# A decoder layer's feed forward: low parts of the right factors on GpSimd, output shares two units later, two last outputs from ScalarE's queue

## The chip, the core and the metric

One core of a Trainium2 chip runs the whole kernel in one launch. The metric is the device time of one execution in microseconds; the median of several runs counts. The engines are TensorE (PE; its weight loads are PEld), VectorE (DVE), ScalarE (ACT), GpSimd (POOL) and SyncE (SP), whose queue issues nearly all DMAs.

## The reference

One inference step of a decoder layer, for a prompt of 512 tokens and 8 sample tokens, with a width of 1024. All is float32.

```python
def run_trunk(x, pos, ...):
    mix, s_new, kvs = token_mixer(rmsnorm(h, ln1_g), pos, ...)
    h = h + mix
    h = h + swiglu(rmsnorm(h, ln2_g), w_ffn_in, w_ffn_out)
    y = rmsnorm(h, lnf_g)

def swiglu(xn, w_ffn_in, w_ffn_out):
    a, b = jnp.split(xn @ w_ffn_in, 2, axis=-1)
    return (jax.nn.silu(a) * b) @ w_ffn_out
```

The mixer (retention, dilated window attention, gates) fills the first 930 us of the kernel. The change lies in `swiglu`, whose hidden width is 2816 (22 blocks of 128), and in the final norm.

## The kernel before, in words

All activations stand transposed, channels on partitions, the 520 tokens as columns in two halves of 260. Every float32 product is made of three products of rounded parts: a value is split into a high part, rounded by ScalarE (`A.activation(..., AF.Copy)` into the type fp32r), and a low part, value minus high part, by VectorE; the three products are high by high, high by low and low by high. The weights come from `wall` in the order of use, 512 KB a DMA on SP's queue, are split the same way (`wh` by `block_hi` at L201, `wl` at L204) and run some five blocks ahead of TensorE (`advance`).

The feed forward goes by units, one for each of the 22 hidden blocks. A plain unit (`ffn_in`) makes the two products `a` and `b` one after the other, 96 matmuls of 128x260. The others, listed in `INQ`, are quads (`ffn_in_quad`): the two output blocks, the two token halves and pairs of weight blocks are taken as a 2x2 product made with seven block products in place of eight, 84 matmuls. Each quad needs three sums of weights from VectorE (`block_sum`, L185, L189 and L191), which are then split as well, and factors of the activations on the right. The seven blocks of a quad go to three PSUM banks: blocks 1, 3, 5, 7 to one, 2 and 6 to another, 4 to a third (`SEVEN`). After blocks 1, 2, 3 and 5 ScalarE copies the bank to SBUF (`s`, L313), since the next block of that bank adds to it; a block therefore waits for that copy. VectorE evacuates the rest: `fa` at L1368 after blocks 4 and 6, `uf` at L1376 after block 7.

The hidden activations `uf` of two neighbouring units are what the output products read. `right(b, k)` makes the right factors of a pair: four VectorE instructions make the sums `us`, and three pieces (`uf`, 780 columns; `us`, 520 columns, twice) are split, high parts `UH` by ScalarE at L1314, low parts `UL` by VectorE at L1318. It is a generator on the track `"S"`; each `pump` of the matmul loop lets it take one step, so its instructions are strewn over the unit after.

The hidden blocks stand in three chunks of 8, 8 and 6 (`CHUNKS`). When a chunk is done, its share of the output is made: four quads `ffn_out(0)`, `(2)`, `(4)`, `(6)`, each adding to two blocks of `hT`. `FFSEQ` gives the order. The shares of a chunk stand one unit behind its last unit, so that `right` has that unit to run in: units 0 to 8, four shares, units 9 to 16, four shares, units 17 to 21, then the last chunk's outputs in plain products (`LAST`), whose factors `whole` splits without sums. Units 7, 8, 9, 11, 12, 13, 15, 16, 17, 19, 20 and 21 are quads.

Right factors of a full pair are made behind the odd units 3, 5, 7, 9, 11, 13 and 15 and, for the first pair, behind unit 2. Units 3 to 6 run beside `gen_factors`, which makes the quads' factors of the normalised input (`XP`, `XT`) on VectorE and ScalarE.

At the end, `fin_out(f)` scales the rows of each token half and stores them: for each of two column halves, row block `j` even by VectorE, `j` odd by ScalarE, each followed by a DMA on SP's queue, then the small `y_s`.

Of the kernel before, what the change touches and what calls it, by code (L numbers as in the profile page):

```python
# [11 lines left out]
ALU = mybir.AluOpType  # L12
# [10 lines left out]
NFF = 22  # L23
# [4 lines left out]
INQ = (7, 8, 9, 11, 12, 13, 15, 16, 17, 19, 20, 21)  # L28
FFSEQ = []
for (a_, n_), ahead_ in zip(CHUNKS, (1, 1, 0)):  # L30
    FFSEQ += [("in", i_, i_ in INQ) for i_ in range(a_ and a_ + 1, a_ + n_ + ahead_)]
    FFSEQ += [("out", c_, True) for c_ in range(0, 8, 2) if ahead_]
QUADS = {128 + 2 * i_: 4 for i_, e_ in enumerate(FFSEQ) if e_[2]}
SCW = (8, 7, 7, 6)
# [4 lines left out]
def tile_hybrid_layer(  # L39
# [9 lines left out]
    V, A, G_, PE, SP = nc.vector, nc.scalar, nc.gpsimd, nc.tensor, nc.sync  # L49
# [13 lines left out]
    def halves(ap):  # L63
        return ap.rearrange("p (f c) -> p f c", f=2)
# [10 lines left out]
    def f32(ap):  # L75
        return ap.bitcast(F32)
# [28 lines left out]
    def later(n, fn):  # L105
        delayed.append([n, fn])
# [31 lines left out]
    def push(name, gen):  # L138
        tracks[name].append(gen)
        return gen  # L140

    def finish(name, gen):
        while gen in tracks[name]:
            run_delayed()
            step(name)
# [140 lines left out]
    def quad(factor, snap, evac):  # L286

        s = pos[0] // 8
        pos[0] += 16
        nkp = QUADS[s]  # L290

        turn["busy"] ^= 1
        pms = {}
        for _ in range(2):
            i = turn["next"]
            pms[i] = bank_pair(i)[:, 0, :HF]
        out = [pms[turn["busy"]], pms[1 - turn["busy"]], None]
        begun = set()
        for j, (bank, x) in enumerate(SEVEN):
            advance(bid[s, 0] + j)  # L300
            if bank == 2:
                out[2] = abank("pc")[:, :HF]
            h, l = split[bid[s, 0] + j]
            for k in range(nkp):
                ks = slice(k * 128, k * 128 + 128)
                for w, i in ((h, 0), (h, 1), (l, 0)):
                    PE.matmul(out[bank], w[:, ks], factor(i, k, x), start=bank not in begun, stop=k == nkp - 1 and w is l,  # L307
                              skip_group_check=True)
                    begun.add(bank)
                if k % 2:  # L310
                    pump()
            if j in (0, 1, 2, 4):
                A.activation(snap[(0, 3, 1, None, 2)[j]], out[bank], AF.Copy)  # L313
            evac(j, out[bank])
# [12 lines left out]
    def rstd_rows(pool, ssq, rows, ncol, n, tag):  # L327

        v = pool.tile([128, 8], F32, tag=tag + "v", bufs=2, name="v")
        V.tensor_scalar(v[:rows, :ncol], ssq, 1.0 / n, EPS, op0=ALU.mult, op1=ALU.add)  # L330
        r = pool.tile([128, 8], F32, tag=tag + "r", bufs=2, name="r")
        G_.tensor_tensor(r[:rows, :ncol], v[:rows, :ncol], mhalf[:rows].to_broadcast([rows, ncol]), op=ALU.pow)  # L332
        return r
# [831 lines left out]
    def ftmp(name):  # L1165
        return fp.tile([128, C], F32, tag="t", bufs=5, name=name)
# [101 lines left out]
    UF = {}  # L1268
    NP = CHUNKS[2][0]
    NX = 3  # L1270

    def snaps():
        return [fp.tile([128, 2, HF], F32, tag=t, bufs=b, name=t) for t, b in (("s12", 1), ("s35", 1))]

    def whole(i, t):
        hi, lo = (halves(u[:, i - NP, :]) for u in (UHp, ULp))
        A.activation(hi, t, AF.Copy)
        later(2, lambda: V.tensor_tensor(lo, t, f32(hi), op=ALU.subtract))

    def middle(i, mult):  # L1280

        if i > NP:
            t = halves(ftmp("fu"))
            mult(t)
            whole(i, t)
            return
        if i % 2 == 0:
            if len(rights) > 1:
                finish("S", rights[-2])
            UF[i // 2] = fp.tile([128, 4, HF], F32, tag="uf", bufs=2, name="uf")  # L1290
        t = UF[i // 2]
        mult(t[:, 1:3, :] if i % 2 else t[:, 0::3, :])
        if i == NX - 1:
            rights.append(push("S", right(UF[0], 0)))
        if i % 2 and i > NX - 1:
            rights.append(push("S", right(t, i % 8 // 2)))

    rights = []

    def right(b, k):  # L1300

        yield
        t = fp.tile([128, 4, HF], F32, tag="us", name="us")
        V.tensor_tensor(t[:, 0, :], b[:, 0, :], b[:, 3, :], op=ALU.subtract)
        yield
        V.scalar_tensor_tensor(t[:, 1, :], b[:, 2, :], -1.0, t[:, 0, :], op0=ALU.mult, op1=ALU.subtract)
        yield
        V.tensor_tensor(t[:, 2, :], b[:, 2, :], b[:, 3, :], op=ALU.subtract)
        yield
        V.scalar_tensor_tensor(t[:, 3, :], t[:, 1, :], -1.0, b[:, 1, :], op0=ALU.mult, op1=ALU.subtract)  # L1310
        yield
        for x, j, n in ((b[:, 0:3], 0, 3), (t[:, 0:2], 3, 2), (t[:, 2:4], 5, 2)):
            hi, lo = (u[:, k, j:j + n, :] for u in (UH4, UL4))
            A.activation(hi, x, AF.Copy)  # L1314
            yield
            if k < 3:
                yield
            V.tensor_tensor(lo, x, f32(hi), op=ALU.subtract)  # L1318
            if k < 3:
                yield  # L1320

# [60 lines left out]
    def ffn_out(c):  # L1382

        s12, s35 = snaps()
        h1, h2 = halves(hT[:, c, :]), halves(hT[:, c + 1, :])

        def evac(j, bank):
            if j == 3:
                V.tensor_tensor(h1[:, 0, :], bank, h1[:, 0, :], op=ALU.add)
                later(1, lambda: V.tensor_tensor(h1, h1, s12, op=ALU.add))  # L1390
            elif j == 4:
                later(1, lambda: V.tensor_tensor(s35[:, 0, :], s35[:, 0, :], s35[:, 1, :], op=ALU.add))
            elif j == 5:
                V.tensor_tensor(h1[:, 1, :], bank, h1[:, 1, :], op=ALU.add)
                V.tensor_tensor(h2[:, 1, :], h2[:, 1, :], s35[:, 0, :], op=ALU.subtract)
            elif j == 6:
                V.tensor_tensor(h2[:, 0, :], h2[:, 0, :], bank, op=ALU.subtract)

        quad(ufactor, [s12[:, 0, :], s12[:, 1, :], s35[:, 0, :], s35[:, 1, :]], evac)

    for kind, i, seven in FFSEQ:
        if kind == "out":
            if i == 0:
                finish("S", rights[-1])
            ffn_out(i)
            continue
        if i == NP + 1:
            whole(NP, UF[NP // 2][:, 0::3, :])
        (ffn_in_quad if seven else ffn_in)(i)

    last = bpool.tile([128, 7 * D], F32, tag="bg", name="last")
    yt = last[:, :4 * D].rearrange("p (j c) -> p j c", j=4)
# [4 lines left out]
    def fin_T(c, f):  # L1417
        h = hT[:, c, :]
        sp, sp2 = sbank(), sbank()
        for j in range(2):  # L1420
            o = f * HF + 128 * j
            pe_T(sp[:, j * 128:(j + 1) * 128], h[:, o:o + 128])
        pe_T(sp2[:4, :128], h[:, f * HF + HT:(f + 1) * HF])
        return sp, sp2

    def fin_ss(f, sq, first):
        for j in range(2):
            PE.matmul(ssb[:, 2 * f + j:2 * f + j + 1], sq[:, 128 * j:128 * j + 128], ones1, start=first and f + j == 0,
                      stop=not first, skip_group_check=True)
        PE.matmul(ssb[:4, 4 + f:5 + f], sq[:, HT:HF], ones1, start=False, stop=not first, skip_group_check=True)  # L1430
# [28 lines left out]
    def fin_out(f):  # L1459
        sq = ftmp("sqf")  # L1460
        A.activation(sq[:, :HF], hT[:, 7, f * HF:(f + 1) * HF], AF.Square)
        fin_ss(f, ssa[:, f * HF:(f + 1) * HF], True)
        a = fin_T(7, f)
        fin_ss(f, sq, False)
        r = rstd_rows(fp, ssb[:, 2 * f:2 * f + 2], 128, 2, D, "nf")
        r4 = rstd_rows(fp, ssb[:4, 4 + f:5 + f], 4, 1, D, "ng")
        fin_g(7, f, *a)
        for i in range(2):
            cs = slice(512 * i, 512 * i + 512)
            for j in (2 * f, 2 * f + 1):  # L1470
                if j % 2:
                    A.activation(yt[:, j, cs], yt[:, j, cs], AF.Copy, scale=r[:, 1:2])
                else:
                    V.tensor_scalar(yt[:, j, cs], yt[:, j, cs], r[:, 0:1], None, op0=ALU.mult)
                SP.dma_start(y_p[0, j * 128:(j + 1) * 128, cs], yt[:, j, cs])
        V.tensor_scalar(ys[:, f, :], ys[:, f, :], r4[:4, 0:1], None, op0=ALU.mult)
        SP.dma_start(y_s[4 * f:4 * f + 4].rearrange("r o d -> r (o d)"), ys[:, f, :])

# [26 lines left out]
    for f in range(2):  # L1505
        for c in range(4, 8):
            o = free_pair()[:, :1, :]
# [120 lines left out]
```

## Time and profile before

| | us |
|---|---|
| median of 3 runs (lowest to highest) | 1306.59 (1304.96 to 1307.02) |
| the profiled execution's own time | 1305.23 |
| its span, first to last instruction | 1303.4 |
| TensorE busy in the span | 1276.1 |
| VectorE busy | 821.0 |
| ScalarE busy | 573.5 |
| GpSimd busy | 83.6 |

The granted TensorE clock is 0.996 of full speed over the span. The profile is of one execution. The timeline lists instructions of one engine in order, with start and length in us and, in brackets, the idle time ahead and what ended it. Matmuls are pipelined: each is shown with some 0.28 us and the next starts 0.12 us later, so that an idle time shown ahead of a matmul is some 0.16 us less than the time that the stream lost. VectorE's instructions overlap a little at their ends; what one costs is the step from its start to the next one's.

### The profile page before, as it was taken

What the parts mean: (1) busy time and instruction counts of PE and PEld (TensorE: products, weight loads), DVE (VectorE), ACT (ScalarE), POOL (GpSimd) and SP (SyncE); (2) the same over time, 40 slices, a digit from 0 to 9 for tenths busy, and PEclk for the clock granted to TensorE, in tenths of its full rate; (3) what the DMA queues carried; (4) which work ended last, traced back from release to release, by engine and by line L of the source; (5) the groups of instructions that cost most, each with busy time, mean ns of one, the idle gap of its engine ahead of it and who ended that gap; (6) DMA issues with size and microseconds to landing.
All of it is one profiled execution on the core that took longest, in us unless ns stands there. A gap on an engine that the chain in (4) does not pass through costs nothing.

```text
span 1303.4 us, 25688 instructions
## 1 busy us (share of the span) xinstructions
PE 1276.1 (98%) x10465; PEld 1245.0 (96%) x10465; DVE 821.0 (63%) x1737; ACT 573.5 (44%) x1100; POOL 83.6 (6%) x69
## 2 busy tenths in 40 slices
PE   8999999999999999999999999999999999999997
PEld 7999999999898999999999999899999999999997
DVE  7866636847765532234545455476688988798765
ACT  4465334635563522244434343233354555555542
POOL 3601001001002000000000000040000000000000
PEclk8999999999999999999999999999999999999999
DMA  6266344746584332435555545624222333233321
GB/s 213 93 208 230 119 158 140 250 153 230 171 292 149 98 95 84 138 122 159 159 150 157 160 149 189 222 98 147 82 82 82 98 112 100 87 93 113 98 82 66
DMA packets 89782, 183.35 MB, mean 141 GB/s; under 512 B 12024, under 2 KB 33944, under 8 KB 89664
## 3 DMA queue, kind: packets, MB, share of 16 engines
q1 hardware_dynamic: 88944, 180.64, 43.0%
q8 instruction: 82, 1.34, 0.4%
q10 hardware_dynamic: 720, 1.07, 0.3%
q14 instruction: 36, 0.29, 0.1%
HBM read 155.70 MB, written 25.98 MB: 139 GB/s over the span
## 4 chain that ended last, share of the span: by engine, by line
PE 85%; DVE 6%; DMA 3%; issue 2%; ACT 2%; POOL 1%; SPq 1%; DVEq 0%; ACTq 0%
PE pm L251 61%; PE pm L307 10%; PE sp L323 3%; PE pc L307 2%; PE sp L553 2%; DVE wl L204 2%; PE sp L572 1%; DMA vb<-vd 1%; PE pm L1516 1%; PE sp L968 1%; ACT wh L201 1%; PE sp L505 1%; DMA out<-st 1%; PE sp L918 1%; PE sacc L1113 1%
## 5 line engine op out<-in xcount | busy, mean ns | idle before, releaser
L251 PE MATMUL pm<-X,wh 128*128 128x260 f32 x3392 | 560.9, 287 | 4.4 <-DVE X L355 3.6
L251 PEld LDWEIGHTS pm<-X,wh 128*128 128x128 f32 x3392 | 469.5, 189 | 18.9 <-issue 9.1
L204 DVE TENSOR_TENSOR wl<-raw,wh 128x512 fp32r<-128x512 f32 x384 | 274.4, 716 | 165.0 <-ACT wh L201 161.6
L251 PE MATMUL pm<-X,wl 128*128 128x260 f32 x1696 | 342.3, 283 | 0.0
L201 ACT ACTIVATE wh<-raw 128x512 fp32r<-128x512 f32 x384 | 238.7, 625 | 210.7 <-PE pm L251 163.5
L251 PEld LDWEIGHTS pm<-X,wl 128*128 128x128 f32 x1696 | 262.5, 189 | 0.1
L251 PE MATMUL pm<-GA,wh 128*128 128x260 f32 x512 | 82.2, 283 | 0.0
L307 PE MATMUL pm<-XT,wh 128*128 128x260 f32 x384 | 71.5, 285 | 1.4 <-DVE uf L1376 1.2
L251 PE MATMUL pm<-XP,wh 128*128 128x260 f32 x448 | 71.9, 283 | 0.0
L251 PEld LDWEIGHTS pm<-GA,wh 128*128 128x128 f32 x512 | 70.1, 188 | 0.0
L307 PEld LDWEIGHTS pm<-XT,wh 128*128 128x128 f32 x384 | 59.1, 188 | 3.0 <-DVE uf L1376 2.0
L251 PEld LDWEIGHTS pm<-XP,wh 128*128 128x128 f32 x448 | 61.3, 188 | 0.0
L307 PE MATMUL pm<-UH,wh 128*128 128x260 f32 x192 | 54.6, 284 | 3.9 <-DVE fa L1368 2.8
L332 POOL TENSOR_TENSOR r<-v,cst 128x4 f32<-128x4 f32 (+4 forms) x14 | 17.6, 1261 | 598.0 <-DVE v L330 598.0
L307 PE MATMUL pm<-UH,wl 128*128 128x260 f32 x192 | 54.3, 283 | 0.0
L307 PE MATMUL pm<-UL,wh 128*128 128x260 f32 x192 | 54.3, 283 | 0.0
L307 PE MATMUL pm<-XT,wl 128*128 128x260 f32 x192 | 54.1, 282 | 0.0
L658 DVE SCALAR_TENSOR_TENSOR st<-st,kv 128x512 f32<-128x512 f32 x64 | 45.5, 714 | 13.3 <-ACT kv L623 11.5
L623 ACT ACTIVATE kv<-vb,ks 128x512 f32<-128x512 f32 x64 | 44.0, 714 | 22.0 <-DMA vb<-vd 20.8
L251 PE MATMUL pm<-GA,wl 128*128 128x260 f32 x256 | 51.6, 283 | 0.0
L313 ACT ACTIVATE s<-pm 128x260 f32<-128x260 f32 x80 | 30.9, 387 | 46.7 <-PE pm L307 46.4
L201 ACT ACTIVATE wh<-qq 128x512 fp32r<-128x512 f32 x60 | 37.0, 626 | 24.2 <-PE pm L251 11.6
(324 smaller groups left out, 2097.0 us busy)
## 6 DMA issues: line engine op xcount, KB each, us to landing
raw<-wall SPq DMA_DIRECT2D x192, 512.0 KB
st<-state SPq DMA_DIRECT2D x64, 256.0 KB
out<-st SPq DMA_DIRECT2D x64, 256.0 KB
area<-ck SPq DMA_DIRECT2D x24, 512.0 KB
vb<-vd SPq DMA_DIRECT2D x32, 256.0 KB
area<-qd SPq DMA_DIRECT2D x12, 512.0 KB
cb<-cd SPq DMA_DIRECT2D x4, 768.0 KB
xr<-xT SPq DMA_DIRECT2D x8, 260.0 KB
```

Source lines behind the costliest of these rows:

```text
L201: A.activation(h, r, AF.Copy)
L204: V.tensor_tensor(l, r, f32(h), op=ALU.subtract)
L251: PE.matmul(pm[:, f, :HF], w, x[f] if isinstance(x, tuple) else x[:, f * HF:(f + 1) * HF], start=first, stop=last)
L307: PE.matmul(out[bank], w[:, ks], factor(i, k, x), start=bank not in begun, stop=k == nkp - 1 and w is l, skip_group_check=True)
L313: A.activation(snap[(0, 3, 1, None, 2)[j]], out[bank], AF.Copy)
L323: PE.transpose(out, in_, ident[:n, :n])
L332: G_.tensor_tensor(r[:rows, :ncol], v[:rows, :ncol], mhalf[:rows].to_broadcast([rows, ncol]), op=ALU.pow)
L505: PE.matmul(sp[:, :T - i0], x[:, dt, jb * 128:(jb + 1) * 128], y[:, dt, i0:], start=i == 0, stop=i == len(mm) - 1)
L553: PE.matmul(sp[:, i0:], v[x][:, jb, c * 128:(c + 1) * 128], scs[y][:, SCO[jb]:SCO[jb] + T - i0], start=jb == 0 and x == y, stop=jb == 3 an ...
L572: PE.matmul(sp, kt[x][:, jb, dt * 128:(dt + 1) * 128], v[y][:, jb, :], start=jb == 0 and x == y, stop=jb == 3 and x == 1)
L623: A.activation(kvs[i][:, :DV], vbs[b], AF.Copy, scale=ks[:, dt, b:b + 1])
L658: V.scalar_tensor_tensor(sts[i], sts[i], GAMMA[h], kvs.pop(i)[:, :DV], op0=ALU.mult, op1=ALU.add)
```

## The change

Three things. The low parts of the right factors are made by GpSimd (`G_`) in place of VectorE. The shares of the first two chunks stand two units behind their last unit in place of one: units 0 to 9, four shares, units 10 to 17, four shares, units 18 to 21. For that, the factors of the pair that ends in unit 9 (`FIRSTS`) are made only when the fourth share has been issued, since they overwrite those of the chunk before, and the same holds for the plain splits of units 16 and 17. And of the last token half the two outputs of the odd row block are issued from ScalarE's queue.

```diff
--- before.py
+++ after.py
@@ -28,7 +28,7 @@
 INQ = (7, 8, 9, 11, 12, 13, 15, 16, 17, 19, 20, 21)
 FFSEQ = []
 for (a_, n_), ahead_ in zip(CHUNKS, (1, 1, 0)):
-    FFSEQ += [("in", i_, i_ in INQ) for i_ in range(a_ and a_ + 1, a_ + n_ + ahead_)]
+    FFSEQ += [("in", i_, i_ in INQ) for i_ in range(a_ and a_ + 2, min(a_ + n_ + 2, NFF))]
     FFSEQ += [("out", c_, True) for c_ in range(0, 8, 2) if ahead_]
 QUADS = {128 + 2 * i_: 4 for i_, e_ in enumerate(FFSEQ) if e_[2]}
 SCW = (8, 7, 7, 6)
@@ -1279,7 +1279,7 @@
 
     def middle(i, mult):
 
-        if i > NP:
+        if i > NP + 1:
             t = halves(ftmp("fu"))
             mult(t)
             whole(i, t)
@@ -1292,10 +1292,11 @@
         mult(t[:, 1:3, :] if i % 2 else t[:, 0::3, :])
         if i == NX - 1:
             rights.append(push("S", right(UF[0], 0)))
-        if i % 2 and i > NX - 1:
+        if i % 2 and i > NX - 1 and i not in FIRSTS:
             rights.append(push("S", right(t, i % 8 // 2)))
 
     rights = []
+    FIRSTS = (9, 17)
 
     def right(b, k):
 
@@ -1315,7 +1316,7 @@
             yield
             if k < 3:
                 yield
-            V.tensor_tensor(lo, x, f32(hi), op=ALU.subtract)
+            G_.tensor_tensor(lo, x, f32(hi), op=ALU.subtract)
             if k < 3:
                 yield
 
@@ -1398,14 +1399,21 @@
 
         quad(ufactor, [s12[:, 0, :], s12[:, 1, :], s35[:, 0, :], s35[:, 1, :]], evac)
 
+    n_out = 0
     for kind, i, seven in FFSEQ:
         if kind == "out":
             if i == 0:
                 finish("S", rights[-1])
             ffn_out(i)
+            if i == 6:
+                o = FIRSTS[n_out]
+                n_out += 1
+                if o > NP:
+                    whole(NP, UF[NP // 2][:, 0::3, :])
+                    whole(NP + 1, UF[NP // 2][:, 1:3, :])
+                else:
+                    rights.append(push("S", right(UF[o // 2], 0)))
             continue
-        if i == NP + 1:
-            whole(NP, UF[NP // 2][:, 0::3, :])
         (ffn_in_quad if seven else ffn_in)(i)
 
     last = bpool.tile([128, 7 * D], F32, tag="bg", name="last")
@@ -1472,7 +1480,7 @@
                     A.activation(yt[:, j, cs], yt[:, j, cs], AF.Copy, scale=r[:, 1:2])
                 else:
                     V.tensor_scalar(yt[:, j, cs], yt[:, j, cs], r[:, 0:1], None, op0=ALU.mult)
-                SP.dma_start(y_p[0, j * 128:(j + 1) * 128, cs], yt[:, j, cs])
+                (A if f and j % 2 else SP).dma_start(y_p[0, j * 128:(j + 1) * 128, cs], yt[:, j, cs])
         V.tensor_scalar(ys[:, f, :], ys[:, f, :], r4[:4, 0:1], None, op0=ALU.mult)
         SP.dma_start(y_s[4 * f:4 * f + 4].rearrange("r o d -> r (o d)"), ys[:, f, :])
```

How this moves instructions, at three places. Names with a number are one buffer: `raw`, `qq` hold weights and their sums, `wh`, `wl` the split weights.

First, unit 8, which carries the `right` of units 6 and 7. VectorE's instructions from its running sum of weights on (minus is before, plus now):

```order
 L185 TENSOR_TENSOR qq_12221<-raw_12076,raw_12078 128x1024
-L1310 SCALAR_TENSOR_TENSOR us<-us,uf 128x260
+L1311 SCALAR_TENSOR_TENSOR us<-us,uf 128x260
 L204 TENSOR_TENSOR wl_12224<-raw_12076,wh_12223 128x512
 L189 TENSOR_TENSOR raw_12078<-raw_12076,qq_12221 128x512
-L1318 TENSOR_TENSOR UL<-uf,UH 128x780
 L204 TENSOR_TENSOR wl_12244<-qq_12221,wh_12243 128x512
-L1318 TENSOR_TENSOR UL<-us,UH 128x520
-L1368 TENSOR_TENSOR fa<-pc,s_12174 128x260
-L1318 TENSOR_TENSOR UL<-us,UH 128x520
+L1369 TENSOR_TENSOR fa<-pc,s_12174 128x260
```

The three low parts leave VectorE's order and the rest moves up; they stand on GpSimd now, alone in its queue, each waiting for its high part. ScalarE's instructions at the same place:

```order
 L201 ACTIVATE wh_12243<-qq_12221 128x512
-L1314 ACTIVATE UH<-us 128x520 x2
+L1315 ACTIVATE UH<-us 128x520 x2
 L201 ACTIVATE wh_12265<-raw_12078 128x512
 L313 ACTIVATE s_12175<-pm 128x260
 L201 ACTIVATE wh_12283<-raw_12078 128x512
-L1370 ACTIVATE fa<-fa 128x520
```

Nothing moves here but the line number. The split of the summed weights `raw_12078` stands ahead of the copy `s_12175` of the bank of block 5.

Second, TensorE at the end of unit 8, before:

```order
L307 MATMUL pm<-XT,wh_12198 128x260 x2
L307 MATMUL pm<-XT,wl_12199 128x260
L307 MATMUL pm<-UH,wh_12223 128x260
L307 MATMUL pm<-UL,wh_12223 128x260
L307 MATMUL pm<-UH,wl_12224 128x260
```

and now:

```order
L307 MATMUL pm<-XT,wh_12198 128x260 x2
L307 MATMUL pm<-XT,wl_12199 128x260
L307 MATMUL pm<-XP,wh_12223 128x260 x2
L307 MATMUL pm<-XP,wl_12224 128x260
L307 MATMUL pm<-XP,wh_12223 128x260 x2
```

Behind the last block of unit 8 came the first block of the first share, which reads `UH` and `UL`; now it is the first block of unit 9, which reads the input's factors.

Third, ScalarE's last instructions, now:

```order
L1453 ACTIVATE sqf<-hT 128x260 x2
L1469 ACTIVATE sqf<-hT 128x260
L1480 ACTIVATE last<-last,r 128x512
L1483 DMA out<-last 128x512
L1480 ACTIVATE last<-last,r 128x512
L1483 DMA out<-last 128x512
```

Before, the two scalings (L1472) stood last without the DMAs, which SP issued.

## Rows read from the trace of the kernel before

**Rows 1.** The page, part 1: busy time (share of the span) and instructions.

```profile
PE 1276.1 (98%) x10465; PEld 1245.0 (96%) x10465; DVE 821.0 (63%) x1737; ACT 573.5 (44%) x1100; POOL 83.6 (6%) x69
```

**Rows 2.** Waits of TensorE from 860 us on: total, times, longest.

```profile
PE pm L307 <- DVE fa L1368: 3.6, 3, 1.4
PE pm L307 <- DVE uf L1376: 2.3, 3, 1.2
```

**Rows 3.** Timeline of TensorE (start, length, idle before and releaser); PEld loads weights.

```profile
1028.24 0.39 PE L307 MATMUL pm<-UH,wh 128*128 128x260 f32 x1 [1.40 <-DVE fa L1368]
1030.49 0.39 PE L307 MATMUL pm<-UH,wh 128*128 128x260 f32 x1 [0.55 <-DVE uf L1376]
1112.39 0.51 PE L307 MATMUL pm<-XP,wh 128*128 128x260 f32 x2 [0.78 <-DVE fa L1368]
1115.26 0.51 PE L307 MATMUL pm<-XT,wh 128*128 128x260 f32 x2 [1.16 <-DVE uf L1376]
1017.95 0.30 PEld L307 LDWEIGHTS pm<-XT,wh 128*128 128x128 f32 x2 [0.21 <-DVE uf L1376]
```

**Rows 4.** Timeline of VectorE in unit 8.

```profile
1020.50 1.21 DVE L185 TENSOR_TENSOR qq<-raw,raw 128x1024 f32<-128x1024 f32 x1
1022.58 0.68 DVE L189 TENSOR_TENSOR raw<-raw,qq 128x512 f32<-128x512 f32 x1
1023.18 0.96 DVE L1318 TENSOR_TENSOR UL<-uf,UH 128x780 fp32r<-128x780 f32 x1
1024.66 0.69 DVE L1318 TENSOR_TENSOR UL<-us,UH 128x520 fp32r<-128x520 f32 x1
1025.61 0.69 DVE L1318 TENSOR_TENSOR UL<-us,UH 128x520 fp32r<-128x520 f32 x1
1027.76 0.42 DVE L1368 TENSOR_TENSOR fa<-pm,s 128x260 f32<-128x260 f32 x1
```

**Rows 5.** Timeline of VectorE and GpSimd where the gated branches are merged.

```profile
859.67 0.69 DVE L1148 TENSOR_TENSOR M<-sgat,M 128x520 fp32r<-128x520 f32 x1
859.84 1.70 POOL L1146 TENSOR_TENSOR sgat<-sgat,sgbt 128x520 f32<-128x520 f32 x1 [1.17 <-DVE sgbt L1145]
860.28 1.80 DVE L204 TENSOR_TENSOR wl<-raw,wh 128x512 fp32r<-128x512 f32 x1
862.01 0.68 DVE L1145 TENSOR_TENSOR sgbt<-sgbt,pm 128x520 f32<-128x520 f32 x1
```

**Rows 6.** Timeline of both where GpSimd adds alone.

```profile
103.96 0.75 DVE L564 SCALAR_TENSOR_TENSOR GT<-sp,vec,g 128x512 f32<-128x512 f32 x1 [0.73 <-ACT sq L562]
104.06 1.29 POOL L563 TENSOR_TENSOR ssa<-ssa,sq 128x512 f32<-128x512 f32 x1 [34.32 <-ACT sq L562]
```

**Rows 7.** Timeline of ScalarE and TensorE in unit 8; 1108.20 is in unit 12.

```profile
1020.50 0.85 ACT L1314 ACTIVATE UH<-uf 128x780 fp32r<-128x780 f32 x1
1024.00 0.39 ACT L313 ACTIVATE s<-pm 128x260 f32<-128x260 f32 x1
1108.20 0.63 ACT L201 ACTIVATE wh<-raw 128x512 fp32r<-128x512 f32 x1 [0.99 <-DVE raw L189]
1025.24 0.40 PE L307 MATMUL pm<-XT,wh 128*128 128x260 f32 x2
```

**Rows 8.** Timeline in units 3 to 5; the last is busy time by stretch.

```profile
975.59 0.69 DVE L1349 TENSOR_TENSOR uf<-pm,fa 128x520 f32<-128x520 f32 x1
986.72 0.69 DVE L1349 TENSOR_TENSOR uf<-pm,fa 128x520 f32<-128x520 f32 x1
989.23 0.60 ACT L1339 ACTIVATE fa<-pm 128x520 f32<-128x520 f32 x1 [2.44 <-PE pm L251]
...
963.00:1000.00 37.00, 37.00 (x311) 37.00 (x310) 36.76 (x70) 18.28 (x31) 0.00 (x0) 1.00 0.28 86
```

**Rows 9.** Timeline of the last outputs; the last column counts merged instructions.

```profile
1297.51 1.33 ACT L1472 ACTIVATE last<-last,r 128x512 f32<-128x512 f32 x2 [1.79 <-POOL r L332]
1298.03 1.81 SPq L1475 DMA_DIRECT2D out<-last  x4
```

## The prediction

> **What bounds the kernel now.** The page's busy lines come first [rows 1]: TensorE is busy 98% of the span. So only what makes TensorE stand still is worth time, and that is looked for where the change acts, in the feed forward (from about 930 us). The waits of TensorE from 860 us on [rows 2] name VectorE alone: 3.6 us for the evacuation `fa` and 2.3 us for `uf`, three times each. The timeline of TensorE shows where [rows 3]: at the joint behind unit 8 (1.40 and 0.55 us idle) and at the joint between units 12 and 13 (0.78 and 1.16). The joint behind unit 16 repeats the first to the hundredth. That is 5.84 us in all, and these three quads are the ones into which `right` is spread. A joint behind a quad without `right` costs only 0.21 us, at its second block (last row of rows 3).
>
> VectorE's timeline in unit 8 says why [rows 4]. It runs without a pause there, and three low parts of the right factors (`UL`) stand ahead of the late `fa`. By start to start they take 0.88, 0.61 and 0.61 us, 2.10 in all; without them `fa`, at 1027.76, would start at 1025.66, when its block is just done. So what the change takes from VectorE is the right thing, if it costs VectorE nothing elsewhere.
>
> **GpSimd beside VectorE.** It does cost. The only dense stretch before the change with GpSimd on 128x520 operands is the merge of the gates [rows 5]. GpSimd's add is asked for at 859.84, behind a VectorE subtraction that runs until about 860.25, and ends at 861.54: it waited 0.4 us and ran 1.29 us. The next VectorE subtraction, of two operands in SBUF, takes 1.80 us in place of 0.69, and the one after it starts 1.73 us later in place of 0.61. The neighbour loses 1.12 us to one GpSimd operation. The two alternate: GpSimd gets its turn at the end of the running VectorE instruction, ahead of the next one. Alone, a 128x512 add takes 1.29 us, and a VectorE instruction beside it with one operand in PSUM keeps its 0.75 us [rows 6]: only instructions with both operands in SBUF are held up.
>
> [...]
>
> So one `right` gives VectorE 2.10 us back and takes 1.12 us for each 128x520 part. The 128x780 part has no row: 1.29 x 780 / 512 = 1.97 us as an estimate, a loss of about 1.8 us; the ends are 1.1 us (no longer than 520 columns) and 2.6 us (1.70 x 1.5, the row with its wait in it). I take 1.8, as the larger operand is nearest to the scaled row. Together 4.0 us: VectorE loses 1.9 us a `right`, where it had no pause. No row has GpSimd writing the rounded type that `UL` has; I take the same time, and the upper end covers it.
>
> The Trainium skill (GPSIMD Engine Reference, 2.1 Instruction dispatch) gives about 2.5 cycles an element at 1.2 GHz for two inputs, an estimate of 1.63 us for 780 columns; by it the sum below would be some 1.5 us less over its five places. No run here shows that operation yet.
>
> **Part 1, low parts on GpSimd, in the three quads.** Unit 8, followed row by row. ScalarE ends the first high part about 1021.35; GpSimd takes its turn when the running sum of weights L185 ends, about 1021.65 [rows 4, 7], and holds until 1023.6. VectorE's next row, `us` L1310, comes after it, some 1.9 us late. The last high part needs that `us`, so it moves to about 1024.6. GpSimd's second part runs 1023.97 to 1025.27, one VectorE row follows, the third part runs 1025.87 to 1027.17. Only then comes the sum of weights L189, which stood at 1022.58: done at 1027.8 in place of 1023.26. ScalarE's next row splits that sum (rows 7 show it waiting for L189 in unit 12), and the copy `s` of the fifth block's bank stands behind it: it moves from 1024.00 to 1028.4. The seventh block of unit 8, which began at 1025.24 [rows 7], adds into that bank and so cannot start before 1028.8: TensorE stands 3.55 us. Then five VectorE rows remain before the late `fa`, which ends at 1030.67; the seventh block ends at 1030.24, so the joint costs 0.46 more, and the second block behind it 0.75 in the manner of the 0.55 there now. The sum is 4.76 us in place of 1.95: +2.8. Unit 16 has the same order: +2.8 again.
>
> In unit 12 the parts lie further apart (k below 3 has more pauses). The first hold, 1.9 us, falls ahead of L189, for which ScalarE waits at 1108.20 [rows 7]; `s` behind it moves as far, and had some 0.4 us to spare: 1.5 us at the seventh block. The other two parts lie ahead of the late `fa` with what is left of the first: 2.5 us at the joint, where 0.78 stands now. Then 0.7 at the second block. 4.7 in place of 1.94: +2.8. The three make +8.4 us.
>
> **Part 1, in the plain units.** In units 3 to 5 VectorE runs all but without a pause from 963 to 1000 us, and its evacuation `uf` is late but not too late [rows 8]: unit 4 ends at 983.3 (two half units of 5.75 us back from the end of unit 5), its `uf` starts at 986.72, and its bank pair is wanted again at 989.05, where the first half of unit 5 ends. The slack is 1.65 us there and 1.25 us for the `uf` at 975.59. The first `right` takes 1.9 of it, 0.7 too much; the second another 1.9, about 1.5 too much. +2.2 us, between 0 (ScalarE's high parts late enough to spread them) and 4. Units 6, 10 and 14 have pauses of 2 to 3 us on VectorE, which cover 1.9; without them each would cost up to 1.9.
>
> **Part 2, shares two units later.** Units 9 and 17 move in front of the shares, and their `right` or split is held back until the fourth share is issued. No work is added: before, that `right` ran in unit 10 too. The low parts of units 7 and 15 get 10 us more before they are wanted, which hides GpSimd's latency, but not its holds. What is added is a joint quad to quad and quad to share in place of quad to share and share to quad: 0.21 us each [rows 3], +0.4 for two. The weights' loads keep their order and pace.
>
> **Part 3, last outputs.** SP issues its four outputs in 1.81 us, one every 0.45 us [rows 9]. Two of them move to ScalarE's queue, behind each of its two 0.7 us scalings. The first issue holds the second scaling by some 0.4 us, so ScalarE issues the last one at about 1299.4, where SP issued it before at 1299.44. Only the small `ys` output gains, some 0.9 us, and it isn't alone at the end. I take -0.1, between -0.9 (the small output alone sets the end) and +0.4 (one issue more on ScalarE).
>
> **Sum:** +8.4 + 2.2 + 0.4 - 0.1 = +10.9 us on the span, of which the alternation of rows 5 carries most. A replay by hand tends to take every collision; where ScalarE or TensorE waits too, a hold meets an idle VectorE. I take 10 us. The profiled execution has a span of 1303.4 and a time of 1305.23 us, 1.36 under the median of 1306.59: 1305.2 + 10 = 1315.2, or 1316.6 from the median. I say **1316**. What 0.2% is here, 2.6 us, is about what a measurement of this kernel can tell from no change.
>
> **Rivals.**
> - *Relief*: GpSimd works beside VectorE without holding it, or only when it rests. Then the 2.10 us are won at each of the three places: the joints fall from 5.84 us to three of 0.21, and 0.4 is added: -4.8, and -0.1 for the tail: 1301.7 by the median. For it: `fa` is late by just the 2.1 us that go. Against it: the 1.80 us row. It decides where GpSimd's hold costs VectorE under 0.6 us a part. Chance 0.12.
> - *A draw*: the holds fall behind L189 or into VectorE's pauses, so that each part costs about what it cost on VectorE: +0.4, +1 for the plain units: 1308. For it: the first hold must come before L189 by only 1 us. Against it: in unit 8 ScalarE's high part is ready 1 us before. Chance 0.14.
> - *A longer hold*: the rounded output or the 780 columns make the parts as long as 1.70 and 2.55 us throughout: 1.4 us more for each of five places, +17: 1323. For it: no row shows that output on GpSimd. Against it: steady 1.29 us alone. Chance 0.12.
>
> **How the numbers follow.** The forecast has 0.62, its own range 1311 to 1320. Faster by over 0.2% is the relief and little else: 0.13. Within 0.2% lies most of the draw: 0.10. Slower 0.77. The range 1305 to 1323 leaves out the relief and the far end of the long hold.
>
> **What would show it.** Right: rows of the splits L204 and sums L185, L189 near 1.8 us or more beside GpSimd's `UL`; TensorE idle 1.5 to 3.5 us ahead of the seventh block of units 8, 12 and 16, waiting for `s`; waits for `uf` in units 4 and 5; a tail as long as before. Wrong: VectorE rows near 0.69 us beside `UL`, and joints of 0.2 us; then the relief holds.

## The result and the profile after

The changed kernel takes 1313.51 us (median of 4 runs, 1313.11 to 1313.95). The kernel before, run beside it again, has a median of 1305.78. The ratio is 1.0062, with a 95% interval of 1.0045 to 1.008: slower, by 7.7 us from median to median. The span of the profiled execution grew from 1303.4 to 1311.7 us.

The page, part 1 (busy time, share of the span, instructions), of the changed kernel; TensorE's line answers to [rows 1]:

```profile
PE 1278.8 (97%) x10465; PEld 1245.6 (95%) x10465; DVE 832.2 (63%) x1713; ACT 573.2 (44%) x1100; POOL 127.4 (10%) x93
```

TensorE has the same 10465 matmuls. VectorE lost 24 instructions and is yet busy for 11.2 us more (821.0 before). GpSimd got the 24 and 43.8 us. The 24 took 8 x 2.10 = 16.8 us of VectorE's time before, so the instructions that were left to it have become some 28 us longer.

TensorE's waits from 860 us on, which answer to [rows 2] (total, times, longest):

```profile
PE pm L307 <- ACT s L313: 7.1, 4, 2.9
PE pm L307 <- DVE fa L1369: 1.7, 1, 1.7
PE pm L251 <- DVE uf L1350: 1.6, 2, 1.1
PE pm L307 <- DVE uf L1377: 0.6, 1, 0.6
```

`fa` and `uf` of the quads made 5.9 us before and make 2.3 now, but a wait for ScalarE's copy `s` is new, 7.1 us, and one for `uf` of the plain units, 1.6 us.

Unit 8, in order of time, on four engines (answers to [rows 4] and [rows 7]):

```profile
1022.68 2.04 POOL L1319 TENSOR_TENSOR UL<-uf,UH 128x780 fp32r<-128x780 f32 x1 [15.83 <-ACT UH L1315]
1022.89 2.12 DVE L1311 SCALAR_TENSOR_TENSOR us<-us,uf 128x260 f32<-128x260 f32 x1
1024.68 3.19 POOL L1319 TENSOR_TENSOR UL<-us,UH 128x520 fp32r<-128x520 f32 x2
1024.93 1.80 DVE L204 TENSOR_TENSOR wl<-raw,wh 128x512 fp32r<-128x512 f32 x1
1026.65 1.76 DVE L189 TENSOR_TENSOR raw<-raw,qq 128x512 f32<-128x512 f32 x1
1028.59 0.63 ACT L201 ACTIVATE wh<-raw 128x512 fp32r<-128x512 f32 x1 [2.91 <-DVE raw L189]
1029.12 0.37 ACT L313 ACTIVATE s<-pm 128x260 f32<-128x260 f32 x1
1029.54 0.51 PE L307 MATMUL pm<-XT,wh 128*128 128x260 f32 x2 [2.88 <-ACT s L313]
1030.82 0.42 DVE L1369 TENSOR_TENSOR fa<-pm,s 128x260 f32<-128x260 f32 x1
```

The collision stands in the rows. GpSimd's 780 columns start some 0.2 us before the running sum of weights ends, and `us` L1311 behind it takes 2.12 us in place of 0.42. The two 520-column parts take 3.19 us together, and beside them the split takes 1.80 us and the sum L189 1.76, in place of 0.68 each. ScalarE waits 2.91 us for that sum, splits it, and only then copies `s` (1029.12); TensorE, which wants that copy for the seventh block, stood 2.88 us. The late `fa` at 1030.82 is no longer what is waited for: the seventh block still runs then. Unit 16 shows the same, row by row.

Then comes something that no row of before had. Busy time by stretch; the columns are PE, PEld, DVE, ACT, POOL, granted clock, DMA share, GB/s:

```profile
1026.50:1029.50 3.00, 0.17 (x2) 0.00 (x0) 3.00 (x5) 0.92 (x3) 1.37 (x1) 1.00 0.00 0
1029.50:1034.00 4.50, 4.46 (x24) 4.46 (x25) 3.87 (x9) 2.19 (x4) 0.00 (x0) 0.62 0.24 66
1034.00:1040.00 6.00, 6.00 (x52) 6.00 (x52) 5.00 (x8) 3.35 (x7) 0.00 (x0) 1.00 0.39 128
```

After the idle 3 us TensorE's granted clock is 0.62 in the mean of the next 4.5 us, that is 1.2 GHz in place of 2.4 for some 3.4 of them, and 1.00 again behind. In that time three matmuls take 0.65 us from start to start, in place of 0.36:

```profile
1030.06 0.64 PE L307 MATMUL pm<-XT,wh 128*128 128x260 f32 x2
1030.49 0.42 PE L307 MATMUL pm<-XT,wl 128*128 128x260 f32 x1
1030.71 0.64 PE L307 MATMUL pm<-XT,wh 128*128 128x260 f32 x2
```

So 3.4 us at the lower level cost 1.5. It happens in units 8 and 16 alike; before, the clock was at its upper level all through these stretches (granted clock 1.00 from 1018 to 1034 us).

Unit 12 and the joint behind it on TensorE, and the new joint between unit 9 and the first share (answers to [rows 3]):

```profile
1115.12 0.51 PE L307 MATMUL pm<-XT,wh 128*128 128x260 f32 x2 [1.19 <-ACT s L313]
1118.57 0.51 PE L307 MATMUL pm<-XP,wh 128*128 128x260 f32 x2 [1.74 <-DVE fa L1369]
1120.83 0.51 PE L307 MATMUL pm<-XT,wh 128*128 128x260 f32 x2 [0.55 <-DVE uf L1377]
1044.28 0.19 PEld L307 LDWEIGHTS pm<-UH,wh 128*128 128x128 f32 x1 [0.21 <-DVE uf L1377]
```

1.19 us for the copy, 1.74 for the late `fa`, 0.55 at the second block: 3.48 in place of 1.94. At the new joint TensorE's weight loads stand 0.21 us; its matmuls there start 0.28 us apart in place of 0.12, so the joint costs 0.16.

The units 4 and 5, VectorE's `uf` and TensorE behind it (answers to [rows 8]):

```profile
976.63 0.69 DVE L1350 TENSOR_TENSOR uf<-pm,fa 128x520 f32<-128x520 f32 x1
977.38 0.75 PE L251 MATMUL pm<-XP,wh 128*128 128x260 f32 x4 [0.50 <-DVE uf L1350]
990.20 0.74 PE L251 MATMUL pm<-XP,wh 128*128 128x260 f32 x4 [1.05 <-DVE uf L1350]
```

The `uf` of unit 3 comes at 976.63, and the bank pair that it frees is late by 0.50 us; the next one by 1.05.

**The sum.** An idle time hides 0.16 us more for each stop. Units 8 and 16: 2.88 + 0.16 + 1.5 in place of 1.95 + 0.32, so +2.3 each. Unit 12: 3.48 + 0.48 in place of 1.94 + 0.32: +1.7. The plain units: 1.55 + 0.32: +1.9. Two new joints: 0.16 us each, +0.3. Together +8.5 us, where the span grew by 8.3. Ahead of the feed forward the profiled execution of the changed kernel is 0.8 us early (one matmul starts at 936.35 in place of 937.18), so the feed forward itself grew by some 9 us and the sum leaves about half a microsecond of it unexplained.

### The profile page after: what moved, and what is told of

Its sections match the earlier page's. It is cut to its first block, busy times and chain, and to the rows that moved or that the text cites. A ratio compares the mean times of both kernels' runs of the same rounds, so it can differ in the third digit from the quotient of the medians.

```text
span 1311.7 us, 25712 instructions
## 1 busy us (share of the span) xinstructions
PE 1278.8 (97%) x10465; PEld 1245.6 (95%) x10465; DVE 832.2 (63%) x1713; ACT 573.2 (44%) x1100; POOL 127.4 (10%) x93
## 4 chain that ended last, share of the span: by engine, by line
PE 83%; DVE 7%; DMA 3%; issue 3%; ACT 2%; POOL 1%; SPq 0%; ACTq 0%; DVEq 0%
PE pm L251 59%; PE pm L307 10%; PE sp L323 3%; DVE wl L204 2%; PE pc L307 2%; PE sp L553 2%; PE sp L572 1%; PE pm L1524 1%; DMA out<-st 1%; PE sp L968 1%; ACT wh L201 1%; DMA vb<-vd 1%; PE sp L505 1%; PE sp L918 1%; PE sacc L1113 1%
## 5 line engine op out<-in xcount | busy, mean ns | idle before, releaser
L204 DVE TENSOR_TENSOR wl<-raw,wh 128x512 fp32r<-128x512 f32 x384 | 282.5, 738 | 159.6 <-ACT wh L201 156.5
L204 DVE TENSOR_TENSOR wl<-qq,wh 128x512 fp32r<-128x512 f32 x60 | 43.4, 723 | 7.3 <-ACT wh L201 7.2
```

Source lines behind the costliest of these rows:

```text
L204: V.tensor_tensor(l, r, f32(h), op=ALU.subtract)
```

## The experiments

The theory, called the hold below: GpSimd's subtractions, which read SBUF, make VectorE's instructions with two operands in SBUF stand still while they run, and cost more there than they save. The rivals: the new order costs the time; low parts come too late; ScalarE's queue order is the cause. All ratios are to the kernel before, run beside.

**Low parts on GpSimd alone.** The kernel before with

```diff
-            V.tensor_tensor(lo, x, f32(hi), op=ALU.subtract)
+            G_.tensor_tensor(lo, x, f32(hi), op=ALU.subtract)
```

> The kernel before with the low parts on GpSimd alone; shares one unit later and the tail on SP's queue as before. Theory (hold: each GpSimd subtraction keeps VectorE's two-operand instructions standing while it runs): nearly the whole loss of the change, 1312 to 1314 us, with TensorE idle about 3 us ahead of the seventh block of units 8 and 16. Rival (order: the moved shares cost the time): 1300 to 1302, VectorE relieved. Rival (latency: low parts come too late for TensorE): slower than the whole change, over 1316, with TensorE waiting for GpSimd's UL at the first share.

Measured: 1312.66 us beside 1304.81, ratio 1.0064 (1.0051 to 1.0076). Its waits of TensorE:

```profile
PE pm L307 <- ACT s L313: 7.1, 4, 2.9
PE pm L307 <- DVE fa L1368: 1.7, 1, 1.7
PE pm L251 <- DVE uf L1349: 1.7, 2, 1.1
```

These are the waits of the changed kernel: this one line carries the whole loss. No wait for `UL` shows, so the low parts are not late even with the shares one unit behind.

**Shares two units later alone.** The diff of the change without its GpSimd line and without its tail line.

> The kernel before with the shares two units later alone; low parts on VectorE, tail on SP's queue. Theory (hold): one more joint of 0.2 us in each of two places, and the joints of 1.95 us stay where right runs: 1306 to 1307 us. Rival (order): most of the loss, 1311 or more.

Measured: 1305.12 us beside 1304.81, ratio 1.0001 (0.9993 to 1.001). Its waits of TensorE:

```profile
PE pm L307 <- DVE fa L1369: 3.6, 3, 1.4
PE pm L307 <- DVE uf L1377: 2.3, 3, 1.2
```

They are those of [rows 2] to the tenth: the stalls stay with the work of `right`, and nothing was won or lost that could be measured. The time lies under the 1306 to 1307 us foreseen, as the kernel before did beside it (1304.81).

**The tail alone.** The kernel before with

```diff
-                SP.dma_start(y_p[0, j * 128:(j + 1) * 128, cs], yt[:, j, cs])
+                (A if f and j % 2 else SP).dma_start(y_p[0, j * 128:(j + 1) * 128, cs], yt[:, j, cs])
```

> The kernel before with only the two last outputs on ScalarE's queue. Theory: within 0.3 us of before, 1305.5 to 1306.1, since ScalarE's second issue comes no sooner than SP's fourth did. Rival (the tail was bound by SP's issue): 0.5 to 0.9 us faster. Rival (issue on ScalarE costs): 0.5 slower.

Measured: 1304.68 us beside 1304.81, ratio 1.0001 (0.9992 to 1.0011). The timeline of the changed kernel's last outputs, which answers to [rows 9] (ACTq is ScalarE's queue):

```profile
1306.13 0.82 SPq L1483 DMA_DIRECT2D out<-last  x2
1307.52 0.35 ACTq L1483 DMA_DIRECT2D out<-last  x1
```

ScalarE's second issue, the last row, starts 1.39 us after the first issue of all; SP's fourth before started some 1.4 us after it. The time did not move.

**GpSimd fills in place of subtracting.** The changed kernel with

```diff
-            G_.tensor_tensor(lo, x, f32(hi), op=ALU.subtract)
+            G_.memset(f32(lo), 0.0)
```

> The changed kernel in which GpSimd fills the low parts of the right factors with zeros and reads nothing: the low parts of the hidden activations' right factors are left out of seven products. Theory (hold, by reading): VectorE is relieved of 2.1 us a right and not held, its splits keep 0.69 us, the joints fall to 0.2 us: 1300 to 1302 us. Rival (any GpSimd instruction beside VectorE holds it): 1305 to 1311, VectorE rows over 1 us beside the fills. Rival (order): 1311 or more.

Measured: 1300.19 us beside 1304.81, ratio 0.9963 (0.9948 to 0.9977). No subtraction is made, so the low parts are left out of the products. What TensorE still waits for in the quads, and then a stretch in which fills run without a pause (six of them in the window):

```profile
PE pm L307 <- DVE uf L1377: 0.5, 1, 0.5
```

```profile
1079.73 3.35 POOL L1319 MEMSET UL<- 128x520 f32 x6 [0.20 <-PE pm L307]
1080.20 1.22 DVE L185 TENSOR_TENSOR qq<-raw,raw 128x1024 f32<-128x1024 f32 x1
1081.34 0.69 DVE L204 TENSOR_TENSOR wl<-raw,wh 128x512 fp32r<-128x512 f32 x1
1082.28 0.68 DVE L189 TENSOR_TENSOR raw<-raw,qq 128x512 f32<-128x512 f32 x1
```

Beside the fills VectorE's sums and splits keep their 1.22, 0.69 and 0.68 us. The fills depend on no high part and so ran in other places than the subtractions (around 935 and 1080 us): this run shows what VectorE's relief is worth with GpSimd out of its way, 4.6 us, and, separately, that a filling GpSimd does not hold two-operand instructions.

**GpSimd repeats what VectorE did.** The kernel with the shares moved alone, and

```diff
             V.tensor_tensor(lo, x, f32(hi), op=ALU.subtract)
+            G_.tensor_tensor(lo, x, f32(hi), op=ALU.subtract)
```

> Shares two units later, low parts on VectorE as before, and each repeated by GpSimd right behind (the same values once more). VectorE is neither relieved nor is anything new waited for. Theory (hold): each right costs VectorE 4.0 us more than in the kernel with the shares moved alone; on top of the 1305.1 us of that kernel some 3 x 4 us in the quads and 2 to 6 in the plain units: 1316 to 1324 us. Rival (the loss of the change comes from low parts that are late, not from holds): 1305 to 1307.

Measured: 1324.62 us beside 1305.52, ratio 1.015 (1.0134 to 1.0165). TensorE's waits, and VectorE beside the repeated parts in unit 8:

```profile
PE pm L307 <- DVE fa L1370: 12.2, 3, 4.9
...
1032.27 2.03 DVE L1319 TENSOR_TENSOR UL<-us,UH 128x520 fp32r<-128x520 f32 x1
1034.22 1.76 DVE L204 TENSOR_TENSOR wl<-raw,wh 128x512 fp32r<-128x512 f32 x1
1035.91 1.50 DVE L1374 TENSOR_TENSOR s<-s 128x260 f32<-128x260 f32 x1
```

The values were there already and no wait of TensorE names GpSimd, and yet it costs 19.1 us, 0.6 over the range foreseen. Even the sum `s` of 260 columns, 0.42 us alone, takes 1.50. This is the hold without any relief. Not all of the 19.1 us is standing: in this trace TensorE's granted clock is at the lower level for some 17 us of the feed forward (0.57 from 981 to 985 us, 0.51 from 1035.9 to 1042.8 and from 1172.4 to 1179.3); in the changed kernel it is so for 6.8.

**ScalarE's copy first.** The changed kernel with, in `quad`,

```diff
-            advance(bid[s, 0] + j)
+            if j != 4:
+                advance(bid[s, 0] + j)
...
+            if j == 4:
+                advance(bid[s, 0] + j)
```

behind the copy.

> The changed kernel with ScalarE's copy of the fifth block's bank put ahead of the split of the summed weights in each quad. Theory (hold): the 2.9 us ahead of the seventh block of units 8 and 16 go, and come back at the joint, where TensorE then waits for the late fa, some 4 us behind its block: 1311 to 1314 us, unchanged within 2 us. Rival (the order of ScalarE's queue is the cause, the holds would fit): the joints stay at 0.2 to 0.6 us and the time falls to 1306 or less.

Measured: 1322.63 us beside 1305.52, ratio 1.0135 (1.0117 to 1.0152): slower by some 9 us than foreseen. Its waits of TensorE:

```profile
PE pm L308 <- DVE fa L1372: 8.5, 3, 3.2
PE pm L308 <- DVE uf L1380: 3.9, 7, 0.6
PE pm L308 <- ACT s L314: 0.2, 1, 0.2
```

The wait for `s` is gone (7.1 to 0.2 us) and the one for the late `fa` has taken its place (1.7 to 8.5), as the theory has it: the copy was only the first to be late behind a held VectorE. What was missed is the price of the edit itself: two splits now come together ahead of the late `fa` in every quad, with or without `right`, and joints that cost 0.2 us cost more (`uf` waits in seven places). The clock has a part in it too: the trace is of the shortest of the four executions, 1320.11 us at a mean granted clock of 0.996, and the others took 1322.17 to 1325.54 at 0.993 to 0.990. So the wait moved as foreseen, and the time decides nothing: how much of it is the edit, and whether ScalarE's order has a share in the loss, this run leaves open.

**Half the pace, low parts on GpSimd and on VectorE.** Both from the changed kernel, the second with the subtraction back on VectorE (`V`); `right` behind units 7, 11 and 15 takes a step at every second pump and so lies over two quads:

```diff
-            rights.append(push("S", right(t, i % 8 // 2)))
+            rights.append(push("S", right(t, i % 8 // 2, i in (7, 11, 15))))
...
+    def right(b, k, slow=False):
+        for _ in right_steps(b, k, slow):
+            yield
+            if slow:
+                yield
```

(`right_steps` is the old `right`, with the pauses of k below 3 where it is slow.) On GpSimd:

> The changed kernel with right behind units 7, 11 and 15 taking a step at every second pump, so that it is spread over two quads. Theory (hold): VectorE needs 2 x 8.3 + 1.4 + 4.0 = 22 us in two quads of 20.2: part of the loss stays, 1306 to 1311 us. Rival (the collision with one sum of weights is all): 1301 to 1303.

Measured: 1305.43 us beside 1305.52, ratio 1.0002 (0.9993 to 1.0011). Its waits of TensorE:

```profile
PE pm L307 <- DVE uf L1384: 3.7, 5, 0.9
PE pm L251 <- DVE uf L1357: 1.6, 2, 1.2
```

Spread out, the holds cost much less, a little less than foreseen: five waits of at most 0.9 us in the quads, and the 1.6 us in the plain units, which the edit doesn't touch.

On VectorE:

> The same pace with the low parts on VectorE. Theory: VectorE needs 2 x 8.3 + 3.5 = 20.1 us in two quads of 20.2, and TensorE's joints fall from 1.95 us to 0.2 to 0.6: 1300 to 1303 us, faster than both kernels. Rival (the stall comes from the order at the joint, not from VectorE's load): 1305, no gain.

Measured: 1299.22 us beside 1305.52, ratio 0.9955 (0.9942 to 0.9967). All that TensorE still waits for from 860 us on, and the stretch of units 8 and 9 (columns as above):

```profile
PE sp L323 <- DVE hT L1500: 1.3, 1, 1.3
PE pm L251 <- DVE fa L1344: 0.5, 1, 0.5
...
1016.00:1042.00 26.00, 25.87 (x212) 25.24 (x211) 24.96 (x45) 17.07 (x35) 0.00 (x0) 1.00 0.38 111
```

The waits of the quads are gone from the list, and TensorE is busy for 25.87 of 26 us. This is faster than both kernels, by 0.8 us more than the range foreseen, and 6.2 us faster than the same pace on GpSimd.

**Half the pace in unit 12 alone, and the better kernel once more.** The first is the kernel before, shares one unit behind, with the generator above and `i == 11`.

> The kernel before with the right behind unit 11 alone at half the pace, spread over units 12 and 13; shares one unit later, low parts on VectorE. Theory (VectorE's load in one quad makes the stall): the joint of 1.94 us between units 12 and 13 falls to 0.2 to 0.4, the two others stay: 2 us faster than before, 1302 to 1304 us. Rival (half pace gains only through the moved shares): no change.

Measured: 1303.06 us beside 1304.11, ratio 0.9989 (0.998 to 0.9998). Its waits of TensorE:

```profile
PE pm L307 <- DVE fa L1375: 2.8, 2, 1.4
PE pm L307 <- DVE uf L1383: 1.1, 2, 0.6
```

Of the three waits for `fa` and for `uf` two are left, the 0.78 and 1.16 us between units 12 and 13 are gone. The time follows by 1 us, less than the 2 foreseen, with an interval that reaches from 0.3 to 2.6 us.

> The kernel with the moved shares, the low parts on VectorE and right at half pace behind units 7, 11 and 15, beside the one above on the same chip: 4 us faster than that one, and 5 to 7 us faster than before.

Measured: 1298.59 us beside 1304.11, ratio 0.9955 (0.9942 to 0.9967): 5.5 us under the kernel before and 4.5 under the one with unit 12 alone.

## Why the prediction was right, and where its terms were off

The direction held, and the measured 1313.51 us lies within the range of 1311 to 1320 around the forecast of 1316; the change cost 7.7 us where 10 were taken. The mechanism is the one named, the hold of rows 5. The total is nearer than its terms: stalls that were priced too high and a fall of the clock that was not foreseen offset each other in part, and that is luck. By its steps:

- **The hold.** 1.29 us for 520 columns and an estimated 1.97 for 780. The rows of GpSimd's new instruction (shortest, median, longest in ns):

```profile
L1319 POOL TENSOR_TENSOR UL<-us,UH x16: 1312/1614/1771, 968.3 to 1159.6; 128x520 fp32r<-128x520 f32 x16
L1319 POOL TENSOR_TENSOR UL<-uf,UH x8: 1880/2039/4104, 966.1 to 1156.2; 128x780 fp32r<-128x780 f32 x8
```

The shortest, without a wait in them, are 1.31 and 1.88 us. The scaled row was near, and the rounded type costs nothing visible: the rival of the longer hold falls. The Trainium skill's 2.5 cycles an element (GPSIMD Engine Reference, 2.1 Instruction dispatch), from which 1.63 us was estimated, is called a floor there; the 1.88 measured here lies above it, so as a price it is too low. By it the sum would have been some 1.7 us less (five times 0.34), where the prediction says 1.5.
- **The turns.** That GpSimd gets its turn at the end of the running VectorE instruction fits the quads of the changed kernel, but not every place. In unit 4

```profile
978.73 4.10 POOL L1319 TENSOR_TENSOR UL<-uf,UH 128x780 fp32r<-128x780 f32 x1 [7.21 <-ACT UH L1315]
```

GpSimd's 780 columns took 4.10 us, and 1.88 where nothing stands in the way: it stood some 2.2 us, while VectorE went through five instructions at their usual 0.42 to 0.70 us. What decides the turn, no run shows.
- **Who is held.** Rows 5 and 6 said two operands in SBUF, and the fills say that GpSimd must read. That agrees with the Trainium skill (SBUF — State Buffer, "Who interferes with whom"), with 0.69 us beside a fill and 1.80 beside a subtraction.
- **The quads.** The place was right, down to the sum L189, ScalarE's split and the copy `s`; the size was not. The seventh block was to start 3.55 us late, and it lost 3.04 (2.88 of idle time and the 0.16 that it hides). The step had counted GpSimd's time in full, 1.95 us and twice 1.3, where the prediction's own price for VectorE was 1.8 and twice 1.12, 4.0 together; from start to start VectorE's three held rows lost 1.70, 1.11 and 1.09, 3.9 together. Behind it, 0.46 and 0.75 us at the joint were foreseen and did not come: TensorE ran at half its clock there, which cost 1.5 us and gave VectorE the time to catch up. So +2.3 a unit in place of +2.8, with the lower clock, a term that the prediction lacks, in the place of the joint. In unit 12: 1.5, 2.5 and 0.7 foreseen, 1.19, 1.74 and 0.55 measured (0.16 more each with what an idle time hides), for the same reason: the held rows there lost 3.75 us together.
- **The plain units.** 0.7 and 1.5 us foreseen, 0.50 and 1.05 measured (0.66 and 1.21 with what an idle time hides). Units 6, 10 and 14 cost nothing, as said.
- **The shares.** +0.4 foreseen; the joints cost 0.16 us each, and alone the part made no measurable difference (1.0001).
- **The tail.** -0.1 foreseen, none measured (1.0001).
- **The relief.** Priced at -4.9 us as a rival, with GpSimd not holding; with GpSimd out of the way it was 4.6. So the price of the stalls was right, and the rival fell on the hold alone.

What stays open: how much of the 1.5 us of the lower clock would have been a stall at the joint otherwise. No run separates the two. An estimate from the rows: at 0.12 us a matmul the seventh block of unit 8 would have ended at about 1031.0, ahead of the late `fa`, which is done at 1031.24; with the `uf` behind it the joint would have cost some 1 us, so the clock itself some 0.5.

## What to carry to other kernels

Before a two-input elementwise instruction goes from VectorE to GpSimd, look for a row in which GpSimd runs beside VectorE: here each 520-column part saved 0.61 us of VectorE's time and cost it 1.12, since VectorE was doing two-operand work in SBUF without a pause. When a busy engine has a peak and not a mean too high, spread the work over the next stage: the slack that two units gave was worth 6 us with the low parts left where they were. An engine whose wait is mended shows the next wait behind it, so follow the queue (sum, split, copy, block) and not the one wait that is named.

## What the runs showed that was not expected

TensorE's clock fell to 1.2 GHz for some 3.4 us after it had stood 2.88 us in units 8 and 16 of the changed kernel (granted clock 0.62 over 4.5 us), and not after its stops of 1.19 and 1.74 us in unit 12. The length of a stop does not settle it, since the same stops went both ways. The kernel with the low parts alone on GpSimd has stops of 1.18 and 1.73 us in unit 12, and there the clock did fall behind them (first row below, columns as above). The kernel with the copy first stood 3.22 us behind unit 8 and kept 1.00, and stood 3.22 us behind unit 16 and fell:

```profile
1119.50:1124.00 4.50, 4.28 (x25) 3.98 (x24) 2.59 (x5) 2.02 (x5) 0.00 (x0) 0.62 0.46 136
...
1032.33 0.50 PE L308 MATMUL pm<-XP,wh 128*128 128x260 f32 x2 [3.22 <-DVE fa L1372]
...
1026.00:1045.00 19.00, 15.22 (x123) 14.60 (x121) 16.10 (x26) 9.58 (x19) 2.91 (x2) 1.00 0.21 58
1167.00:1172.00 5.00, 4.19 (x23) 4.19 (x24) 3.50 (x8) 2.58 (x5) 0.00 (x0) 0.66 0.37 107
```

It differs between executions of one kernel too: six of the kernel with the low parts alone on GpSimd have mean granted clocks from 0.993 to 0.996, and the two at 0.993 and 0.994 are the longest (1314.4 us), the three at 0.996 the shortest (1311.7 to 1311.8). No trace shows where the clock fell in the others. So a fall seen in one trace is not a fixed price of its stop.

GpSimd's low parts made VectorE's other instructions some 28 us longer over the kernel, of which TensorE felt about 8; the rest fell where VectorE had pauses or was paid for by the 16.8 us that left it.
